# One mixer kernel on Trainium2: the convolution's first value and gate weights in turns, in four banks

## The chip, the cores and the metric

The kernel runs on one core of a Trainium2 chip. The metric is the device time of an execution in microseconds (us). The kernel before was run three times: median 685.47 us (684.65 to 685.96). A core has five engines that work side by side and wait for one another by semaphores: TensorE (PE in the profile; its weight loads are PEld), VectorE (DVE), ScalarE (ACT), GpSimd (POOL) and SyncE (SP), which issues the transfers here. Matmuls write into PSUM, a memory of eight banks; everything else lives in SBUF.

## The reference

One decoder block in float32 over 256 tokens of width 1024:

```python
h = rmsnorm(x, norm_mix_g)
x = x + parallel_mixer(h, ...)          # attention heads | Conformer convolution, one w_in, one w_out
h = rmsnorm(x, norm_mem_g)
x = x + memory_cross_attention(h, rmsnorm(mem, mem_norm_g), w_mq, w_mkv, w_mo)
h = rmsnorm(x, norm_ffn_g)
x = x + hierarchical_moe(h, ...)        # top-1 group, top-2 of its 8 experts; 32 experts in all
return rmsnorm(x, final_g)

def conformer_conv(u, b_glu, w_dw, b_dw, ln_g, ln_b):   # u = h @ w_in[:, OFF_C:], width 2 x 512
    a, gate = jnp.split(u + b_glu, 2, axis=-1)
    z = a * jax.nn.sigmoid(gate)
    z = depthwise_causal_conv(z, w_dw, width=31) + b_dw
    return jax.nn.silu(layernorm(z, ln_g, ln_b))
```

The convolution's inputs are two products of h, the value `a` and the gate, each 512 columns of `w_in`. The change is about the first half of these columns, chunk 0, at the very start of the kernel.

## The kernel before, in words

**Tiling.** The 256 tokens are two row blocks of 128. x is normalised block by block (`normed`): square sums on ScalarE (first half of the columns) and VectorE (second half), the reciprocal root, then the scaling, again half on ScalarE and half on VectorE, into `xn`. TensorE transposes `xn` into the tile `ht`, two rows j of the contraction at a time, and `put_split` takes it out of PSUM as two float32r parts: a high part (ScalarE) and a low part, the remainder (VectorE). The contraction of 1024 has eight such rows j. Every matrix product of the mixer is done in three matmuls (`mm3`, lines 414 to 417): high x high, high x low, low x high. Weights are split in the same way by `split`, two rows j a piece: the high part `WH` is a cast on ScalarE (line 409), the low part `WL` a subtraction (line 411), every third on VectorE, the others on POOL. Pieces have five buffers.

**Convolution.** `conv_chunk(c)` multiplies 256 value columns (tiles `pa`, two blocks b) and then 256 gate columns (`pg`) of one chunk, 48 matmuls each. Then ScalarE's sigmoid of the gate (line 534) and VectorE's product with the value (line 535) write `z`. The depthwise convolution runs on VectorE as 31 tap operations for each of four channel blocks, 124 in all (`conv_taps`, lines 507 to 516); the program hands them out between the other work by `some_taps`. After the last one `ysum` adds up the channel blocks; `ln_mean` (line 706) lets TensorE multiply it by ones for the LayerNorm's mean `mu`, and VectorE subtracts it (line 707). The LayerNorm's result enters the output projection (`xo`).

**What comes after.** The products for v (tile `pv`; VectorE takes eight columns of it into `fS`, line 554), q and k, attention, the keys of the memory (`pmk`), its values (`pmv`), the output projection, cross-attention, and the 32 experts in eight groups.

**Weights.** SyncE transfers them in tiles of 1 MB into a ring of buffers in a fixed order (`Ring`); a transfer is issued once its buffer has been freed by the work that read it. In the last two thirds of the run these are the experts' weights, about 192 MB.

**What sets the order.** The program is recorded and a scheduler sets each engine's order from priorities; `tc.high_priority(80)` around the splits lets them go ahead of work recorded up to 80 instructions earlier. Inside `tc.manual_schedule(engines=...)` the named engines keep the order in which the program is written. Each engine then works strictly in its order. `keep_warm` issues matmuls without a use (fillers), 16 of them at the start. PSUM's banks are shared out by tags: `mm` has three banks, `tr` (transposes) and `sc` two each, `acc` one.

Of the kernel before, what the change touches and what calls it, by code (L numbers as in the profile page):

```python
# [11 lines left out]
F32 = mybir.dt.float32  # L12
# [41 lines left out]
NSLOT3 = 2  # L54
NWARM = 13
NWARM2 = 5
NWARM0 = 16


class Ring:  # L60
# [3 lines left out]
    def __init__(self, tc):  # L64
        self.tc = tc
        self.nc = tc.nc
        self.size = {}
        self.first = 0
        self.held = 0
        self.begun = False  # L70
        self.todo = deque()
        self.free = deque()
        self.kept = deque()
        self.live = []
# [28 lines left out]
    def pump(self, limit=1000):  # L103
        while self.todo and limit:
            key, shape, src, within = self.todo[0]
            if within is None:
                pool = next((p for p in self.free if self.size[p] >= math.prod(shape)), None)
                if pool is None:
                    return
                self.free.remove(pool)  # L110
                v = self.view(pool, shape, F32)
                self.live.append((key, v, pool))
                v = v[:, :, :src.shape[2]]
            else:
                v = next(e[1] for e in self.live if e[0] == within[0])[:, :, within[1]]
            limit -= 1
            self.todo.popleft()

            n = 1 if self.begun else 2
            self.begun = True  # L120
            for k in range(0, shape[0], shape[0] // n):
                self.nc.sync.dma_start(v[:, k:k + shape[0] // n], src[:, k:k + shape[0] // n])

    def take(self, key):
        for e in self.live:
# [37 lines left out]
def body(tc, a, out):  # L163
# [31 lines left out]
    def tr_ps(name, shape=(P, 512)):  # L195
        return ps.tile(list(shape), F32, tag="tr", name=name, bufs=2)
# [78 lines left out]
    def qcols(key, view, c0, n):  # L275
        ring.queue(key, (NJ, n), view[:, :, c0:c0 + n])

    for c in range(2):
        qcols(("ca", c), winv, OFF_C + 256 * c, 256)
        qcols(("cg", c), winv, OFF_C + DC + 256 * c, 256)  # L280
    ring.queue(("mem", 0), (NT, D), mem.rearrange("(i p) d -> p i d", p=P))
    for c in range(2):
        qcols(("v", c), winv, OFF_V + VF * c, VF)
# [42 lines left out]
            c0, w = SLICES[2]  # L326
            ring.queue(None, (4, w), wv[:, 3, :, c0:c0 + w], (("ed3", 1), slice(256, 512)))

    ring.pump(2)
    prow = prec.tile([P, P], F32, name="prow")  # L330
    qrow = prec.tile([20, P], F32, name="qrow")
    nc.sync.dma_start(prow[0:124, :], a["w_dw"][0].rearrange("t (c p) -> (t c) p", p=P))
    nc.sync.dma_start(prow[124:128, :], a["b_dw"][0].rearrange("(c p) -> c p", p=P))
    nc.sync.dma_start(qrow[0:8, :], a["b_glu"][0].rearrange("(c p) -> c p", p=P))
    nc.sync.dma_start(qrow[8:12, :], a["conv_ln_g"][0].rearrange("(c p) -> c p", p=P))
    nc.sync.dma_start(qrow[12:16, :], a["conv_ln_b"][0].rearrange("(c p) -> c p", p=P))
    nc.sync.dma_start(qrow[16:20, :], a["attn_out_g"][0].rearrange("(c p) -> c p", p=P))
# [2 lines left out]
    ln_g = qTm[:, 8:12]  # L340
    ln_b = qTm[:, 12:16]
    ao_g = qTm[:, 16:20]
    gain("mem_norm_g", "(p k) -> p k", "mem_norm_g")
    ring.pump(4)
    nc.sync.dma_start(bfor, a["b_forget"][0].partition_broadcast(P))
    ring.first = 1000
    ring.pump()
# [49 lines left out]
    wsp = [None]  # L397
    nsplit = [0]

    def split(v):  # L400

        m = v.shape[2]
        n = 2 * VF // m
        for k in range(0, v.shape[1], n):
            src = v[:, k:k + n]
            with tc.high_priority(AHEAD):
                hi = wsp[0].tile([P, 2 * VF], F32R, tag="WH", name="WH")[:, :n * m].rearrange("p (a b) -> p a b", a=n)
                lo = wsp[0].tile([P, 2 * VF], F32R, tag="WL", name="WL")[:, :n * m].rearrange("p (a b) -> p a b", a=n)
                A.copy(hi, src)  # L409
                nsplit[0] += 1  # L410
                (V if nsplit[0] % 3 == 0 else G).tensor_tensor(lo, src, hi.bitcast(F32), op=OP.subtract)  # L411
            yield [(k + i, hi[:, i], lo[:, i]) for i in range(n)]

    def mm3(o, L, R, first, last):
# [22 lines left out]
    def blocked(k):  # L437
        return slice(k * P, (k + 1) * P)

    def normed(src, dst):  # L440

        for i in range(NT):
            ss = small.tile([P, 2], F32, tag="nrmss", name="nrmss")
            ssq(ss[:, 0:1], src[:, i, :D // 2], A)
            ssq(ss[:, 1:2], src[:, i, D // 2:], V)
            r = small.tile([P, 1], F32, tag="nrmr1", name="nrmr1")
            V.tensor_add(r, ss[:, 0:1], ss[:, 1:2])
            A.activation(r, r, AF.Sqrt, scale=1.0 / D, bias=eps_t)
            V.reciprocal(r, r)
            A.activation(dst[:, i, :D // 2], src[:, i, :D // 2], AF.Copy, scale=r)  # L450
            V.tensor_scalar(dst[:, i, D // 2:], src[:, i, D // 2:], r, None, op0=OP.mult)

    def wstat(key, pair, name, between={}, bank=mm_ps):

# [34 lines left out]
    wst = ExitStack()  # L489
    wsp[0] = wst.enter_context(tc.tile_pool(name="wsp", bufs=NPIECE, side="right", reuse_waits="tile"))  # L490

    normed(X, xn)
    transposed(hT, xn, gvec["norm_mix_g"], 0, NJ, strided, "h")
    ring.done(xn_pool)
    t = tr_ps("prm_t")
    T.transpose(t[:, 0:P], prow, ident)
    T.transpose(t[:, P:P + 20], qrow, ident[0:20, 0:20])
    V.tensor_copy(pT, t[:, 0:P])
    V.tensor_copy(qTm, t[:, P:P + 20])


    z = cvp.tile([P, 4, S + CW - 1], F32, name="z")
    V.memset(z[:, :, 0:CW - 1], 0.0)
# [21 lines left out]
        for _ in range(n):  # L525
            next(taps, None)

    def conv_chunk(c):
        pa = wstat(("ca", c), hT, "pa")
        pg = wstat(("cg", c), hT, "pg")  # L530
        for b in range(2):
            cb = 2 * c + b
            sg = cvp.tile([P, S], F32, tag="sg", name="sg", bufs=2)
            A.activation(sg, pg[b], AF.Sigmoid, bias=b_glu[:, 4 + cb:5 + cb])
            V.scalar_tensor_tensor(z[:, cb, CW - 1:], pa[b], b_glu[:, cb:cb + 1], sg, op0=OP.add, op1=OP.mult)

    conv_chunk(0)
    conv_chunk(1)
    exp_ln = A.preload_act_table_set("natural_log_exp_and_others")
    tc.keep_in_program_order(exp_ln)  # L540

# [835 lines left out]
```

## Time and profile before

| | |
|---|---|
| median of 3 runs | 685.47 us |
| the profiled execution | 686.98 us, its span 685.3 us |
| TensorE busy | 595.5 us, 87% of the span |
| VectorE busy | 224.2 us, 33%, nearly all of it in the first 260 us |
| ScalarE, POOL busy | 173.0 and 119.1 us |
| transfers | 237.35 MB, mean 346 GB/s |

The span is cut into 40 equal slices of 17.1 us in the page. Shares over the whole span say little here, since the mixer and cross-attention fill the first third and the experts the rest; the rows below are therefore taken from single stretches. In the timeline a row has the start, the busy time of the merged instructions, engine, line, operation, the tiles (out<-in), the shape and the count; in brackets stands how long the engine was idle before and what ended that. Matmul durations overlap, so the distance of their starts is what counts.

### The profile page before, as it was taken

The numbers are of one execution on the slowest core, as the hardware profiler recorded it, in microseconds if no ns is written. First come the engines' busy times: TensorE is split into PE (matmuls) and PEld (weight loads), VectorE is DVE, ScalarE is ACT, GpSimd is POOL, SyncE is SP. The second block draws the span as 40 slices with busy tenths as digits, with TensorE's granted clock in tenths as the row PEclk, the third lists the DMA queues.
The fourth block names the chain that finished last, engine by engine and source line by source line (L and its number), as shares of the span: only waits on it lengthen the run. The fifth ranks groups of instructions, "written<-read, shape, count | busy, mean of one in ns | idle before, by whom it ended". The sixth has DMA issues, their size and how long they took to land. (4 is left out here: it accounts for less than half of the span.)

```text
span 685.3 us, 8873 instructions
## 1 busy us (share of the span) xinstructions
PE 595.5 (87%) x3497; PEld 353.1 (52%) x3497; DVE 224.2 (33%) x489; ACT 173.0 (25%) x375; POOL 119.1 (17%) x106
## 2 busy tenths in 40 slices
PE   7999999998999999999768968976895788789775
PEld 5999889876998852625312612521261243125122
DVE  5699879887775630400000100000010000001013
ACT  6576675574654510000000000000000000000004
POOL 4546425674333200000000000000000000000000
PEclk9999999999999999999989989998999899899898
DMA  7979550555966999999999999999999999999993
GB/s 247 358 184 364 209 193 2 184 185 191 361 232 221 395 360 421 420 418 419 420 420 418 421 419 420 419 421 419 421 418 421 419 420 419 421 419 418 421 398 116
DMA packets 65163, 237.35 MB, mean 346 GB/s; under 512 B 11852, under 2 KB 31456, under 8 KB 42080
## 3 DMA queue, kind: packets, MB, share of 16 engines
q1 hardware_dynamic: 64832, 235.72, 87.6%
q10 hardware_dynamic: 288, 1.05, 0.4%
q8 instruction: 28, 0.46, 0.3%
q14 instruction: 15, 0.12, 0.0%
HBM read 235.70 MB, written 1.05 MB: 345 GB/s over the span
## 5 line engine op out<-in xcount | busy, mean ns | idle before, releaser
L1311 PE MATMUL eu<-w,tg 128*32 128x512 f32 x512 | 105.3, 715 | 43.9 <-DMA w<-in_w_up 43.9
L411 POOL TENSOR_TENSOR WL<-w,WH 128x512 fp32r<-128x512 f32 (+1 forms) x80 | 109.2, 1375 | 110.7 <-ACT WH L409 94.9
L1339 PE MATMUL ed<-w,hT 128*32 128x512 f32 x448 | 86.5, 597 | 15.4 <-DMA w<-in_w_down 10.6
L1311 PEld LDWEIGHTS eu<-w,tg 128*32 128x32 f32 x512 | 22.3, 126 | 123.0 <-DMA w<-in_w_up 78.8
L409 ACT CAST WH<-w 128x512 fp32r<-128x512 f32 (+1 forms) x120 | 72.9, 619 | 46.6 <-PE pmk L416 7.3
L998 POOL TENSOR_SCALAR SR<-S,r 128x128 f32<-128x128 f32 x7 | 4.2, 605 | 388.2 <-PE Y L1050 337.3
L1034 DVE TENSOR_TENSOR sgm<-sgm,eu 128x512 f32<-128x512 f32 x8 | 5.5, 688 | 192.7 <-PE eu L1311 164.6
L1016 PEld LDWEIGHTS tgp<-SR,X 128*128 128x128 f32 x256 | 62.0, 335 | 12.0 <-ACT SR L997 9.5
L1016 PE MATMUL tgp<-SR,X 128*128 128x128 f32 x256 | 63.8, 405 | 3.6 <-ACT SR L997 3.6
L1339 PEld LDWEIGHTS ed<-w,hT 128*32 128x32 f32 x448 | 22.2, 109 | 74.6 <-issue 37.4
L512 DVE SCALAR_TENSOR_TENSOR cacc<-z,pT,cacc 128x256 f32<-128x256 f32 x116 | 56.4, 486 | 2.6
L1311 PE MATMUL eg<-w,tg 128*32 128x512 f32 x448 | 53.8, 594 | 0.8 <-DMA w<-in_w_gate 0.8
L1004 DVE TENSOR_TENSOR S<-S,GT 128x256 f32<-128x256 f32 x8 | 3.4, 425 | 126.4 <-POOL SR L998 126.3
L1040 ACT COPY hT<-hTp 128x512 f32<-128x512 f32 x8 | 4.7, 586 | 152.2 <-PE hTp L1037 152.2
L411 DVE TENSOR_TENSOR WL<-w,WH 128x512 fp32r<-128x512 f32 (+1 forms) x40 | 36.4, 911 | 11.0 <-ACT WH L409 10.7
L1033 ACT ACTIVATE sgm<-eg 128x512 f32<-128x512 f32 x8 | 4.8, 597 | 128.3 <-PE eg L1311 112.2
L1311 PEld LDWEIGHTS eg<-w,tg 128*32 128x32 f32 x448 | 16.9, 109 | 30.6 <-issue 22.4
L1048 ACT COPY yd<-ed 128x512 f32<-128x512 f32 x14 | 8.2, 586 | 93.8 <-PE ed L1339 93.8
L1017 DVE TENSOR_TENSOR tg<-tgp,g_norm_ffn_g 128x512 f32<-128x512 f32 (+2 forms) x19 | 11.5, 607 | 53.0 <-PE tgp L1016 53.0
L1050 PE MATMUL Y<-yd,GST 128*128 128x512 f32 x56 | 25.9, 605 | 0.0
L415 PE MATMUL pmk<-w,WH 128*128 128x256 f32 x64 | 18.8, 294 | 0.0
L416 PE MATMUL pmk<-w,WH 128*128 128x256 f32 x64 | 18.5, 290 | 0.0
(353 smaller groups left out, 976.4 us busy)
## 6 DMA issues: line engine op xcount, KB each, us to landing
w<-in_w_gate SPq DMA_DIRECT2D x64, 1024.0 KB, 19.9
w<-in_w_up SPq DMA_DIRECT2D x64, 1024.0 KB, 19.9
w<-in_w_down SPq DMA_DIRECT2D x63, 1024.0 KB, 19.9
w<-in_w_mkv SPq DMA_DIRECT2D x8, 1024.0 KB, 12.8
w<-in_w_in SPq DMA_DIRECT2D x7, 1024.0 KB, 10.5
w<-in_w_out SPq DMA_DIRECT2D x4, 1024.0 KB, 9.4
w<-in_w_mq SPq DMA_DIRECT2D x4, 1024.0 KB, 13.2
w<-in_w_mo SPq DMA_DIRECT2D x4, 1024.0 KB, 5.5
```

The costliest lines, as they stand in the source:

```text
L409: A.copy(hi, src)
L411: (V if nsplit[0] % 3 == 0 else G).tensor_tensor(lo, src, hi.bitcast(F32), op=OP.subtract)
L415: T.matmul(o, L[0], R[0], start=first, stop=False)
L416: T.matmul(o, L[0], R[1], start=False, stop=False)
L512: V.scalar_tensor_tensor(dst, z[:, cb, t:t + S], pT[:, 4 * t + cb:4 * t + cb + 1], acc, op0=OP.mult, op1=OP.add)
L1016: T.matmul(t[:, j], X[:, i, ja + j::NJ], SR[:, i], start=i == 0, stop=i == NT - 1)
L1017: V.tensor_tensor(tg[:, ja:ja + step], t, gff[:, ja:ja + step].unsqueeze(2).to_broadcast([P, step, n]), op=OP.mult)
L1034: V.tensor_mul(sg, sg, pu[0:n])
L1048: ins = A.copy(yd[:, :w], pd[0:n, :w])
L1050: T.matmul(outs[i], GST[:, i], yd[:, :w], start=first, stop=last)
L1311: T.matmul(o[32 * q:32 * q + 32], tg[:, j, 32 * q:32 * q + 32], ws[q][0][:, jj], start=j == 0, stop=j == NJ - 1, tile_position=(0, 32 * q))
L1339: T.matmul(os_[n][32 * q:32 * q + 32], hh[:, j, 32 * q:32 * q + 32], ws[q][0][:, jj, 512 * n:512 * n + 512], start=j == 0, stop=j == 3, ti ...
```

## The change

It does the following.

- The first value and gate weights (`w0`, two ring buffers) are transferred ahead of the rest, each in three pieces of two, two and four rows j, in turns.
- `normed` works on one row block at a time. For block 0 the scaling of the first half of the columns goes from ScalarE to POOL. The sums of block 1 stand behind block 0's on ScalarE.
- On TensorE, VectorE and ScalarE the front is written out by hand: transposes of the first four rows j of block 0, three fillers (of 16; 13 stay at the start), the same of block 1, then pair by pair 12 matmuls of the value and 12 of the gate, each pair's transposes two pairs ahead. Both high parts of a pair precede both low parts (`h_split`). POOL isn't among the engines whose order is written out.
- Value and gate of chunk 0 have four banks (two `mm`, two `sc`). Their low parts go to POOL (value) and to VectorE (gate). Chunk 1's value takes one bank of `mm` and one of `tr`.
- The sigmoids and `z` of chunk 0 come after all 96 matmuls of the chunk.

```diff
-NWARM0 = 16
+NWARM0 = 13
...
-
-            n = 1 if self.begun else 2
-            self.begun = True
-            for k in range(0, shape[0], shape[0] // n):
-                self.nc.sync.dma_start(v[:, k:k + shape[0] // n], src[:, k:k + shape[0] // n])
+            self.nc.sync.dma_start(v, src)
     def take(self, key):
         for e in self.live:
...
     def qcols(key, view, c0, n):
         ring.queue(key, (NJ, n), view[:, :, c0:c0 + n])
-    for c in range(2):
-        qcols(("ca", c), winv, OFF_C + 256 * c, 256)
-        qcols(("cg", c), winv, OFF_C + DC + 256 * c, 256)
+
+    w0 = [ring.spare((NJ, 256)) for _ in range(2)]
+    for j0, j1 in ((0, 2), (2, 4), (4, 8)):
+        for (v, _), c0 in zip(w0, (OFF_C, OFF_C + DC)):
+            nc.sync.dma_start(v[:, j0:j1], winv[:, j0:j1, c0:c0 + 256])
+    for key, c0 in (("ca", OFF_C), ("cg", OFF_C + DC)):
+        qcols((key, 1), winv, c0 + 256, 256)
...
-    ring.pump(2)
+    ring.pump(1)
...
+    ring.pump(2)
-    ring.pump(4)
+    ring.pump(2)
...
-    def split(v):
+    def split(v, eng=None):
...
-                (V if nsplit[0] % 3 == 0 else G).tensor_tensor(lo, src, hi.bitcast(F32), op=OP.subtract)
+                (eng or (V if nsplit[0] % 3 == 0 else G)).tensor_tensor(lo, src, hi.bitcast(F32), op=OP.subtract)
...
-    def normed(src, dst):
-
-        for i in range(NT):
-            ss = small.tile([P, 2], F32, tag="nrmss", name="nrmss")
-            ssq(ss[:, 0:1], src[:, i, :D // 2], A)
-            ssq(ss[:, 1:2], src[:, i, D // 2:], V)
-            r = small.tile([P, 1], F32, tag="nrmr1", name="nrmr1")
-            V.tensor_add(r, ss[:, 0:1], ss[:, 1:2])
-            A.activation(r, r, AF.Sqrt, scale=1.0 / D, bias=eps_t)
-            V.reciprocal(r, r)
-            A.activation(dst[:, i, :D // 2], src[:, i, :D // 2], AF.Copy, scale=r)
-            V.tensor_scalar(dst[:, i, D // 2:], src[:, i, D // 2:], r, None, op0=OP.mult)
+    def normed(i):
+
+        ss = small.tile([P, 2], F32, tag="nrmss", name="nrmss")
+        ssq(ss[:, 0:1], X[:, i, :D // 2], A)
+        ssq(ss[:, 1:2], X[:, i, D // 2:], V)
+        r = small.tile([P, 1], F32, tag="nrmr1", name="nrmr1")
+        V.tensor_add(r, ss[:, 0:1], ss[:, 1:2])
+        A.activation(r, r, AF.Sqrt, scale=1.0 / D, bias=eps_t)
+        V.reciprocal(r, r)
+        if i == 0:
+            G.tensor_scalar(xn[:, i, :D // 2], X[:, i, :D // 2], r, None, op0=OP.mult)
+        else:
+            A.activation(xn[:, i, :D // 2], X[:, i, :D // 2], AF.Copy, scale=r)
...
-    normed(X, xn)
-    transposed(hT, xn, gvec["norm_mix_g"], 0, NJ, strided, "h")
-    ring.done(xn_pool)
-    t = tr_ps("prm_t")
-    T.transpose(t[:, 0:P], prow, ident)
-    T.transpose(t[:, P:P + 20], qrow, ident[0:20, 0:20])
-    V.tensor_copy(pT, t[:, 0:P])
-    V.tensor_copy(qTm, t[:, P:P + 20])
-
     z = cvp.tile([P, 4, S + CW - 1], F32, name="z")
     V.memset(z[:, :, 0:CW - 1], 0.0)
...
-    def conv_chunk(c):
-        pa = wstat(("ca", c), hT, "pa")
-        pg = wstat(("cg", c), hT, "pg")
+    def conv_glu(c, pa, pg):
         for b in range(2):
             cb = 2 * c + b
             sg = cvp.tile([P, S], F32, tag="sg", name="sg", bufs=2)
             A.activation(sg, pg[b], AF.Sigmoid, bias=b_glu[:, 4 + cb:5 + cb])
             V.scalar_tensor_tensor(z[:, cb, CW - 1:], pa[b], b_glu[:, cb:cb + 1], sg, op0=OP.add, op1=OP.mult)
-    conv_chunk(0)
-    conv_chunk(1)
+
+    ht = [None] * (NJ // 2)
+
+    def h_transposes(i, m):
+        if i == 0:
+            ht[m] = tr_ps("ht", (P, 2, S))
+        for kk in range(2):
+            T.transpose(ht[m][:, kk, i * P:(i + 1) * P], xn[:, i, strided(2 * m + kk)], ident)
+
+    def h_split(m):
+        g = gvec["norm_mix_g"]
+        ks = [(kk, 2 * m + kk) for kk in range(2)]
+        for kk, k in ks:
+            A.activation(hT.hi(k), ht[m][:, kk], AF.Copy, scale=g[:, k:k + 1])
+        for kk, k in ks:
+            V.scalar_tensor_tensor(hT.lo(k), ht[m][:, kk], g[:, k:k + 1], hT.hi(k).bitcast(F32),
+                                   op0=OP.mult, op1=OP.subtract)
+
+    def products(o, piece):
+        for b in range(2):
+            bs = slice(b * P, (b + 1) * P)
+            for j, hi, lo in piece:
+                mm3(o[b], (hi[:, bs], lo[:, bs]), hT.both(j), j == 0, j == NJ - 1)
+
+    ET = mybir.EngineType
+    with tc.manual_schedule(engines={ET.PE, ET.Activation, ET.DVE}):
+        normed(0)
+        for m in range(2):
+            h_transposes(0, m)
+        keep_warm(onesb, 3)
+        normed(1)
+        sa, sb = split(w0[0][0], G), split(w0[1][0], V)
+        ap = next(sa)
+        for m in range(2):
+            h_transposes(1, m)
+        pa = [mm_ps("pa", (P, S)) for _ in range(2)]
+        pg = [sc_ps("pg", (P, S)) for _ in range(2)]
+        h_split(0)
+        for m in range(NJ // 2):
+            bp = next(sb)
+            products(pa, ap)
+            if m < NJ // 2 - 1:
+                h_split(m + 1)
+                ap = next(sa)
+            products(pg, bp)
+            if m + 2 < NJ // 2:
+                for i in range(NT):
+                    h_transposes(i, m + 2)
+        t = tr_ps("prm_t")
+        T.transpose(t[:, 0:P], prow, ident)
+        T.transpose(t[:, P:P + 20], qrow, ident[0:20, 0:20])
+        V.tensor_copy(qTm, t[:, P:P + 20])
+        V.tensor_copy(pT, t[:, 0:P])
+        conv_glu(0, pa, pg)
+        ring.done(xn_pool, w0[0][1], w0[1][1])
+
+    banks = cycle((mm_ps, tr_ps))
+    pa = wstat(("ca", 1), hT, "pa", bank=lambda name, shape: next(banks)(name, shape))
```

Where the scheduler and the new code move instructions is seen from the engines' orders. POOL at the start; `WL` is a low part of weights, `w<-X,nrmr` the scaled half of x, `BR` and `iotag` small tables. Before:

```order
L225 CAST Ub<-U 128x128
L249 MEMSET BR 128x40
L252 IOTA iotag 128x32
L411 TENSOR_TENSOR WL<-w,WH 128x512 x11
L411 TENSOR_TENSOR WL<-w,WH 128x520 x5
```

After the change, the same place on POOL:

```order
L220 CAST Ub<-U 128x128
L411 TENSOR_TENSOR WL<-w,WH 128x512
L244 MEMSET BR 128x40
L247 IOTA iotag 128x32
L450 TENSOR_SCALAR w<-X,nrmr_238 128x512
L411 TENSOR_TENSOR WL<-w,WH 128x512 x8
```

One low part of the weights moved ahead of the two tables and stands ahead of the new scaling of block 0. TensorE's first transposes wait for that scaling.

VectorE at the end of the taps, from the last three low parts to the subtraction of the mean; `cacc` and `y<-z,pT,cacc` are taps, `pmv` the memory's values. Before:

```order
L512 SCALAR_TENSOR_TENSOR cacc<-z,pT,cacc 128x256 x7
L411 TENSOR_TENSOR WL<-w,WH 128x512
L512 SCALAR_TENSOR_TENSOR cacc<-z,pT,cacc 128x256 x6
L411 TENSOR_TENSOR WL<-w,WH 128x512
L512 SCALAR_TENSOR_TENSOR y<-z,pT,cacc 128x256
L515 TENSOR_TENSOR ysum<-ysum,y 128x256
L730 COPY w<-pmv 128x512
L411 TENSOR_TENSOR WL<-w,WH 128x512
L707 SCALAR_TENSOR_TENSOR y<-mu,y 128x1024
```

After:

```order
L505 SCALAR_TENSOR_TENSOR cacc<-z,pT,cacc 128x256 x7
L411 TENSOR_TENSOR WL<-w,WH 128x512
L505 SCALAR_TENSOR_TENSOR cacc<-z,pT,cacc 128x256 x5
L778 COPY w<-pmv 128x512
L505 SCALAR_TENSOR_TENSOR cacc<-z,pT,cacc 128x256
L411 TENSOR_TENSOR WL<-w,WH 128x512
L505 SCALAR_TENSOR_TENSOR cacc<-z,pT,cacc 128x256 x2
L505 SCALAR_TENSOR_TENSOR y<-z,pT,cacc 128x256
L508 TENSOR_TENSOR ysum<-ysum,y 128x256
L755 SCALAR_TENSOR_TENSOR y<-mu,y 128x1024
```

The second low part of the upper piece is the first of the lower one. Up to it the order has 123 taps before and 115 after; behind it stand nine taps instead of one, and the copy of `pmv` and a low part moved ahead of `ysum`. Between the first `z` and the first `fS` the count of taps is 39 before and 31 after, and there is one low part less. On TensorE the order from the first product of chunk 1 on is the same in both kernels, but for one matmul.

## Rows read from the trace of the kernel before

**Rows 1.** The page's 40 slices: GB/s of all transfers.

```profile
GB/s 247 358 184 364 209 193 2 184 185 191 361 232 221 395 360 421 420 418 419 420 420 418 421 419 420 419 421 419 421 418 421 419 420 419 421 419 418 421 398 116
```

**Rows 2.** Windows: stretch, length, each engine's busy us (count), PEclk, DMA share, GB/s.

```profile
210.00:215.00 5.00, 5.00 (x29) 4.28 (x28) 2.90 (x6) 3.29 (x8) 2.59 (x2) 1.00 0.33 128
```

**Rows 3.** Waits of SyncE's queue: for whom, us in total, times, longest.

```profile
SPq L122 <- PE eg L1290: 16.8, 4, 8.3
```

**Rows 4.** Waits of TensorE, 26 to 260 us: us in total, times, longest.

```profile
PE xo L417 <- DVE w L720: 1.5, 1, 1.5
PE pq L415 <- DVE fS L554: 0.7, 1, 0.7
```

**Rows 5.** Timeline of the front, four engines: start us, busy us, engine, instruction.

```profile
7.08 0.16 DVE L447 TENSOR_TENSOR nrmr<-nrmss 128x1 f32<-128x1 f32 x1 [0.27 <-ACT junkA L382]
...
8.42 1.12 ACT L409 CAST WH<-w 128x512 fp32r<-128x512 f32 x2
...
9.11 4.21 POOL L411 TENSOR_TENSOR WL<-w,WH 128x512 fp32r<-128x512 f32 x3 [6.33 <-ACT WH L409]
...
9.97 0.50 PE L415 MATMUL pa<-w,WH 128*128 128x256 f32 x2 [0.34 <-ACT w L421]
```

**Rows 6.** Groups by form on POOL: count, busy us, mean ns, idle before.

```profile
L998 POOL TENSOR_SCALAR SR<-S,r 128x128 f32<-128x128 f32 x7 | 4.2, 605 | 388.2 <-PE Y L1050 337.3 <-PE pn L1070 50.9
```

**Rows 7.** Timeline of TensorE: fillers, and transposes at the lower clock.

```profile
1.18 5.92 PE L232 MATMUL warm<-onesb 128*128 128x512 bf16 x16 [1.18 <-POOL onesb L227]
...
12.72 1.09 PE L430 MATMUL ht<-ident,w 128*128 128x128 f32 x4 [0.85 <-DVE w L422]
```

**Rows 8.** Windows: the stretch of the lower clock (PEclk is third from the end).

```profile
12.50:16.50 4.00, 3.78 (x20) 3.81 (x21) 2.55 (x5) 2.40 (x6) 2.09 (x2) 0.57 0.65 192
```

**Rows 9.** Timeline of ScalarE: table load and sigmoid.

```profile
21.15 1.28 ACT L534 ACT_TABLE_LOAD   x1
23.41 0.47 ACT L534 ACTIVATE sg<-pg,qTm 128x256 f32<-128x256 f32 x1 [0.97 <-PE pg L417]
```

**Rows 10.** Timeline: the first z, the gate's second block, the first product of v.

```profile
23.92 0.48 DVE L535 SCALAR_TENSOR_TENSOR z<-pa,qTm,sg 128x256 f32<-128x256 f32 x1 [2.06 <-ACT sg L534]
...
23.93 0.38 PE L415 MATMUL pg<-w,WH 128*128 128x256 f32 x1 [0.56 <-ACT sg L534]
...
39.22 0.28 PE L415 MATMUL pv<-WH,w 128*128 128x260 f32 x1
```

**Rows 11.** Windows: 30 products at the full clock.

```profile
29.21:32.74 3.53, 3.53 (x32) 3.53 (x31) 3.39 (x8) 1.59 (x3) 2.44 (x3) 1.00 1.09 349
```

**Rows 12.** Timeline of VectorE: fS, two waits, the end of the taps.

```profile
52.24 0.17 DVE L554 TENSOR_TENSOR fS<-pv,bfor 128x8 f32<-128x8 f32 x1
...
76.72 0.48 DVE L422 SCALAR_TENSOR_TENSOR w<-mt,g_mem_norm_g,w 128x256 fp32r<-128x256 f32 x1 [2.28 <-ACT w L421]
...
110.60 0.69 DVE L411 TENSOR_TENSOR WL<-w,WH 128x512 fp32r<-128x512 f32 x1 [0.31 <-ACT WH L409]
...
122.31 3.63 DVE L512 SCALAR_TENSOR_TENSOR cacc<-z,pT,cacc 128x256 f32<-128x256 f32 x7
...
129.60 1.25 DVE L411 TENSOR_TENSOR WL<-w,WH 128x512 fp32r<-128x512 f32 x1
...
131.28 1.01 DVE L515 TENSOR_TENSOR ysum<-ysum,y 128x256 f32<-128x256 f32 x1
...
132.82 0.68 DVE L411 TENSOR_TENSOR WL<-w,WH 128x512 fp32r<-128x512 f32 x1
```

**Rows 13.** Groups by form on VectorE, 24 to 53 us: low parts.

```profile
L411 DVE TENSOR_TENSOR WL<-w,WH 128x512 fp32r<-128x512 f32 x3 | 3.1, 1028 | 0.4 <-ACT WH L409 0.4
```

**Rows 14.** Timeline of TensorE: the mean.

```profile
133.62 0.59 PE L706 MATMUL mu<-ysum,ones 128*128 128x256 f32 x2
```

**Rows 15.** Windows: the lower and the full clock behind the LayerNorm.

```profile
161.00:162.00 1.00, 1.00 (x4) 0.71 (x3) 1.00 (x3) 0.52 (x1) 0.41 (x1) 0.50 0.95 315
164.00:165.00 1.00, 1.00 (x6) 0.81 (x5) 0.67 (x1) 0.27 (x1) 0.00 (x0) 1.00 1.05 410
```

More of the change, by code (lines that the diff above doesn't have):

```diff
@@ L69, in __init__ @@
         self.held = 0
-        self.begun = False
         self.todo = deque()
@@ L438, in blocked @@
         return slice(k * P, (k + 1) * P)
-    def normed(src, dst):
-        for i in range(NT):
-            ss = small.tile([P, 2], F32, tag="nrmss", name="nrmss")
-            ssq(ss[:, 0:1], src[:, i, :D // 2], A)
-            ssq(ss[:, 1:2], src[:, i, D // 2:], V)
-            r = small.tile([P, 1], F32, tag="nrmr1", name="nrmr1")
-            V.tensor_add(r, ss[:, 0:1], ss[:, 1:2])
-            A.activation(r, r, AF.Sqrt, scale=1.0 / D, bias=eps_t)
-            V.reciprocal(r, r)
-            A.activation(dst[:, i, :D // 2], src[:, i, :D // 2], AF.Copy, scale=r)
-            V.tensor_scalar(dst[:, i, D // 2:], src[:, i, D // 2:], r, None, op0=OP.mult)
+    def normed(i):
[10 more added lines that the diff above has]
+            A.activation(xn[:, i, :D // 2], X[:, i, :D // 2], AF.Copy, scale=r)
+        V.tensor_scalar(xn[:, i, D // 2:], X[:, i, D // 2:], r, None, op0=OP.mult)
     def wstat(key, pair, name, between={}, bank=mm_ps):
@@ L535, in conv_chunk @@
             V.scalar_tensor_tensor(z[:, cb, CW - 1:], pa[b], b_glu[:, cb:cb + 1], sg, op0=OP.add, op1=OP.mult)
-    conv_chunk(0)
-    conv_chunk(1)
+    ht = [None] * (NJ // 2)
[50 more added lines that the diff above has]
+    pa = wstat(("ca", 1), hT, "pa", bank=lambda name, shape: next(banks)(name, shape))
+    conv_glu(1, pa, wstat(("cg", 1), hT, "pg"))
     exp_ln = A.preload_act_table_set("natural_log_exp_and_others")
```

## The prediction

> **What bounds the kernel now.** I read the page's slices first. From about 255 us to the end the transfers run at their ceiling, about 420 GB/s [rows 1]: there the expert weights decide, and nothing in this change touches them. Before that they are not at the ceiling: between 210 and 215 us they are busy a third of the time [rows 2], because the next weights wait for a buffer that TensorE has yet to free (16.8 us in four waits for its first expert matmuls alone [rows 3]). So a delay of TensorE ahead of 210 us moves every later transfer by as much and arrives at the end in full, and so does a gain. The question is when TensorE gets through the mixer. The next view is what TensorE waits for between 26 and 260 us: very little, and the largest waits are for VectorE [rows 4]. VectorE is the second bound of the mixer: it carries 124 tap operations of the depthwise convolution between its other work, and the LayerNorm behind them ends in the 1.5 us wait.
>
> **The front, up to the first product.** Before, the first product starts at 9.97 us [rows 5]. In the change ScalarE skips one half of the normalisation of row block 0, so its square sum of block 1 starts earlier. VectorE waited 0.27 us for that sum at 7.08 [rows 5], and that is about all that can come earlier: 0.25 us. The first cast (8.42) comes at 8.17, and the low part on POOL (9.11) at 8.86. On POOL this low part now stands ahead of the half that was moved there from ScalarE. So the moved multiplication cannot begin before 8.86 + 1.4 (4.21 us for three [rows 5]) = 10.3, and all transposes of block 0 wait for it. No row has a 128x512 multiplication by a scalar on POOL. Low bound 0.6 us, the one of 128x128 [rows 6]; high bound four times that, 2.4. I take 1.4, the low part of the same size. So block 0 is ready at 11.7 (10.9 to 12.7). The Trainium skill, GPSIMD Engine Reference, 4.1 Engine selection, says that a one-input operation runs there roughly at line rate and a two-input one about half as fast; an estimate from that and the low part's row is 0.7 us, and the sum would be 0.7 us smaller. No row here shows it.
>
> Then TensorE does four transposes, three fillers, four transposes. The fillers are 13 + 3 now. The first 13 end at 1.2 + 13 x 0.37 = 6.0 [rows 7], so TensorE idles 5.7 us. Before, shorter gaps were enough to bring the granted clock to its lower level (1.2 GHz) for most of the 4 us behind 12.5 [rows 8]; I count the restart at that level. Four transposes 1.1 [rows 7], three fillers 1.1, two transposes 0.55, ScalarE's high part 0.5 (the sigmoid's row, of the same shape [rows 9]) and 0.1 of hand-over: 3.3 us, so the first product starts at 15.0, 5.0 us later than before.
>
> **The convolution's first chunk.** Before, from the first product to the first of v it takes 39.22 - 9.97 = 29.25 us [rows 5, 10], though 192 products need only 192 x 0.118 = 22.7 (30 of them in 3.53 us at full clock [rows 11]). The rest are the other transposes, waits for high and low parts, the lower clock, and once in each chunk the wait for a sigmoid that holds the gate's bank (0.56 us shown [rows 10], with the restart about 0.8). The change takes these away: in four banks value and gate alternate by pairs of rows, each pair's high and low part is made during the other's products, and chunk 1 has banks of its own. After: 96 products 11.3, eight transposes 1.1 (half the time of rows 7's each, at full clock), 0.4 for the low part that the first pair waits for (VectorE now makes it second), 0.4 for the rest of the lower clock (0 to 1.2). Chunk 0 ends at 28.2, and v begins 0.3 + 11.3 us later at 39.8, against 39.22. TensorE itself loses only 0.6 us: the stalls removed pay for most of the late start.
>
> **What is late next: VectorE.** Before, the gate b=0 was finished ahead of b=1, so the first z came at 23.92 [rows 10], in the middle of chunk 0. Now both gates end together at 28.2, and behind them come a cast 0.6 [rows 5], a table load 1.3 and a sigmoid 0.5 [rows 9]: z at 30.6, 6.7 us later, and the taps start with it. The order answers by putting taps later. Up to the first fS it has 31 of them where there were 39, and one low part less. A tap takes 3.63/7 = 0.52 us [rows 12], a low part 1.0 [rows 13]. So fS comes 6.7 - 4.1 - 1.0 = 1.6 us later than 52.24 [rows 12]. TensorE waits there already (0.7 us [rows 4]), because fS frees the bank of its next matmul, so this replaces the 0.6: +1.6 at 52 us.
>
> From there VectorE is tied to TensorE and ScalarE again: it waits 2.28 us at 76.7 and 0.31 at 110.6 [rows 12], and since TensorE is 1.6 us late too, those waits remain. The eight taps stay behind. At the low part of 129.60 [rows 12] the order has 115 taps done instead of 123. Behind it stood one tap, the sum ysum, a copy of pmv and a low part; now stand eight more taps, and copy and low part are ahead of the sum. So ysum ends 8 x 0.52 + 1.2 (copy and low part, which ended at 133.5) = 5.3 us later than its 132.29 [rows 12], relative to TensorE. TensorE multiplies it into the mean at 133.62 [rows 14], at a fixed place in its order, with 1.3 us to spare before: it will stand still 4.0 us. Nothing gives that back: the chain from the mean to the LayerNorm's end runs through VectorE and ends in the 1.5 us wait [rows 4], which moves with it.
>
> A stop of 4 us should also lower the clock. Behind the waits for the LayerNorm the granted clock was at the lower level in 161 to 162, four matmuls per us instead of six [rows 15]. At that ratio a low stretch of 3 to 4 us costs 1.0 to 1.3, at half rate 1.7; some of it hides in the later wait for the LayerNorm, so I take 1.0 (0 to 1.7).
>
> **Sum.** Front and fS +1.6, the mean +4.0, the clock +1.0: +6.6 us. The profiled execution took 686.98 us (span 685.3); with it 693.6. It lies 1.5 above the median of 685.47, and the difference carries over: 692.1. The moved DMAs (six pieces instead of three issues ahead of the small tables) cost nothing: the first piece is cast at 8.17 behind ScalarE's own work, the rest is needed after 15; if one came late, the first pair would wait by that much.
>
> **Rivals.**
> VectorE catches up (the other side): it makes up the eight taps in the waits that it still has (2.28 and 0.31 us shown [rows 12], more between), so fS and ysum come in time. Decided by whether ysum ends within 1.3 us of its place; then only TensorE's own 0.6 is left, 686.1, no change. For it: the waits are there. Against: the order is fixed, and a wait ahead of a listed instruction can't be filled by a later tap. 0.11.
>
> The low part doesn't hold POOL's half up, and the front works: first product some 3.5 us earlier, at 11.5. Then z comes at 27.1 and fS 1.9 us earlier than before; but the mean still waits 4.0, since that lag is set by the order and not by the start: 685.5 - 1.9 + 4.0 = 687.6, with the clock 688.6. For it: POOL was idle until 9.11 [rows 5]. Against: POOL's order shows the low part first. 0.12.
>
> The clock stays low longer: 3.5 us more of chunk 0 at half rate add 1.7, and the stop at the mean costs the full 1.7, so 0.7 more: 694.5. For it: the gap of 5.7 us is longer than any that the front had. Against: by the mean of 0.57 over 12.5 to 16.5 [rows 8] the clock was nearly back at the end of that stretch. The Trainium skill, TensorE: Matmul & The Clock Gate, Why this matters for your kernels, warns of idle gaps between bursts of matmuls; on that the trace agrees [rows 8, 15], and this rival is its rule taken at its worst. 0.12.
>
> The forecast: 692.1, own range 690 to 693.5. 0.62. The remaining 0.03 is a gain that I don't see.
>
> **Range and chances.** The forecast's terms with their bounds (block 0 0.8 earlier to 1.0 later, each clock term from 0, the mean 3.5 to 4.7) and most of the second and third rivals give 687.5 to 694.5; the first rival lies outside. About 0.2% (1.4 us) is what a measurement of this kernel can tell from no change. Slower by more than that: 0.62 + 0.12 + 0.12, less a hundredth, 0.85; within it: most of the first rival, 0.10; faster: 0.05.
>
> **What would show it.** In the profile of the changed kernel: POOL's multiplication by nrmr at about 10.3, behind a low part; the first product near 15; no sigmoid wait at the gates; the first z near 30.6; a longer wait for fS near 54; and above all the mean's matmul waiting about 4 us for ysum near 135, with VectorE doing taps right up to it. I am wrong if that wait is under 1 us, or if the transposes of block 0 start by 7 us.

## The result, and the profile after

The changed kernel took 694.55 us (median of 4 runs, 693.64 to 696.43) against 685.72 us for the kernel before on the same chip: ratio 1.0133, 95% interval 1.0106 to 1.0159. It is slower, as forecast, and by more: 692.1 us was predicted, with 694.5 as the upper end. A second session (e1 below) gave 693.15 us and 1.0107 (1.0079 to 1.0136). The executions of one kernel differ by 4 to 6 us, so the two sessions don't contradict each other; the median of all 13 executions of the changed kernel is 694.0. Within a session the changed kernel lies 7.5 to 8.8 us above the kernel before.

The profiled execution took 693.64 us, its span 691.9. In the order of the prediction's steps: the front on POOL and then on TensorE (start us, busy us, engine, instruction, idle time before it and what ended it), which answer [rows 5].

```profile
8.91 1.26 POOL L411 TENSOR_TENSOR WL<-w,WH 128x512 fp32r<-128x512 f32 x1 [6.31 <-ACT WH L409]
10.11 0.13 POOL L244 MEMSET BR<- 128x40 f32 x1
10.19 0.17 POOL L247 IOTA iotag<- 128x32 f32 x1
10.35 1.57 POOL L450 TENSOR_SCALAR w<-X,nrmr 128x512 f32<-128x512 f32 x1
```

```profile
11.97 1.12 PE L535 MATMUL ht<-ident,w 128*128 128x128 f32 x4 [5.55 <-POOL w L450]
12.88 1.48 PE L227 MATMUL warm<-onesb 128*128 128x512 bf16 x3
14.16 1.06 PE L535 MATMUL ht<-ident,w 128*128 128x128 f32 x4
15.36 0.58 PE L415 MATMUL pa<-w,WH 128*128 128x256 f32 x1
```

The low part stands ahead of the scaling on POOL, and all of TensorE's front waits for that scaling. Next, the first z (23.92 before [rows 10]) and fS on VectorE (52.24 before [rows 12]), and the wait for fS on TensorE (0.7 us before [rows 4]).

```profile
31.06 0.48 DVE L526 SCALAR_TENSOR_TENSOR z<-pa,qTm,sg 128x256 f32<-128x256 f32 x1 [1.04 <-ACT sg L525]
```

```profile
54.39 0.17 DVE L602 TENSOR_TENSOR fS<-pv,bfor 128x8 f32<-128x8 f32 x1
```

```profile
54.61 0.39 PE L415 MATMUL pq<-w,WH 128*128 128x256 f32 x1 [1.66 <-DVE fS L602]
```

The end of the taps on VectorE, and the mean on TensorE, which answer [rows 12, 14].

```profile
139.05 0.74 DVE L411 TENSOR_TENSOR WL<-w,WH 128x512 fp32r<-128x512 f32 x1
139.71 1.00 DVE L505 SCALAR_TENSOR_TENSOR cacc<-z,pT,cacc 128x256 f32<-128x256 f32 x2
140.75 0.48 DVE L505 SCALAR_TENSOR_TENSOR y<-z,pT,cacc 128x256 f32<-128x256 f32 x1
141.26 0.42 DVE L508 TENSOR_TENSOR ysum<-ysum,y 128x256 f32<-128x256 f32 x1
```

```profile
136.85 0.40 PE L417 MATMUL pmv<-WH,w 128*128 128x512 f32 x1
141.74 0.70 PE L754 MATMUL mu<-ysum,ones 128*128 128x256 f32 x2 [4.50 <-DVE ysum L508]
```

VectorE works right up to ysum, and TensorE stands still for it: 133.62 before, 141.74 now. Last, windows of TensorE (stretch, length, busy us and count, then PEclk, DMA share, GB/s), which answer [rows 8, 15].

```profile
12.00:16.00 4.00, 3.80 (x12) 0.50 1.10 327
78.00:82.00 4.00, 4.00 (x25) 0.64 0.00 0
142.00:146.00 4.00, 4.00 (x12) 0.57 0.00 0
166.00:170.00 4.00, 2.52 (x11) 1.00 0.26 54
170.00:174.00 4.00, 3.72 (x19) 1.00 0.98 374
```

The lower level (1.2 GHz) stands behind the first wait (12 to 16) and behind the mean's (142 to 146), where a wait stands ahead. It also stands near 78, where TensorE had not waited since 54.6; no step of the prediction had that. At 166 to 174, around the LayerNorm's wait (1.48 us, over at 167.90), the clock is full; in the kernel before that wait ended at 159.09 and a low stretch stood behind it.

The milestones of the traces, each the start of that product in us, with the time of the same execution (pa: the first value product; cps: the first small product behind those for q; pk: the last of those for k; mu: the mean; pp: L1011, see below):

| trace | first pa | first cps | last pk | mu | pp | time |
|---|---|---|---|---|---|---|
| before | 9.97 | 57.52 | 82.32 | 133.62 | 241.32 | 686.98 |
| changed | 15.36 | 59.54 | 85.76 | 141.74 | 249.05 | 693.64 |
| e1 (changed) | 15.23 | 59.42 | 85.66 | 141.65 | 248.91 | 693.29 |
| e14 (changed) | 15.44 | 61.36 | 86.16 | 142.11 | 249.80 | 695.67 |
| e15 (changed) | 15.42 | 61.22 | 86.02 | 141.98 | 249.55 | 694.01 |
| e16 (changed) | 15.40 | 59.60 | 85.79 | 141.76 | 248.94 | 693.05 |
| e2 | 10.16 | 54.35 | 82.07 | 138.04 | 245.29 | 690.50 |
| e3 | 15.22 | 61.49 | 88.47 | 142.92 | 250.04 | 695.29 |
| e4 | 11.64 | 55.83 | 84.34 | 138.77 | 246.59 | 690.62 |
| e5 | 15.37 | 61.77 | 88.00 | 139.55 | 246.11 | 689.98 |
| e6 | 10.03 | 56.65 | 81.45 | 136.08 | 243.86 | 689.12 |
| e7 | 15.27 | 59.56 | 84.28 | 136.90 | 244.40 | 690.36 |
| e8 | 10.28 | 54.39 | 79.17 | 130.97 | 238.58 | 684.09 |
| e9 | 9.51 | 53.71 | 79.93 | 135.89 | 243.12 | 687.90 |
| e10 | 15.44 | 59.64 | 84.44 | 140.39 | 248.11 | 695.96 |
| e11 | 9.96 | 56.38 | 82.60 | 134.15 | 241.20 | 687.29 |
| e12 | 10.31 | 54.54 | 80.85 | 132.64 | 240.25 | 685.26 |
| e13 | 9.62 | 53.70 | 79.92 | 131.76 | 239.23 | 683.42 |

pp is one of the last products ahead of the expert stage. Up to it the changed kernel loses 7.6 to 8.5 us in its five traces, against the one trace of the kernel before; the medians differ by about 8.

### The profile page after: what moved, and what is told of

Same layout as the page of the kernel before. It is cut to its first block, busy times and chain, and to the rows that moved or that the text cites. A ratio compares the mean times of both kernels' runs of the same rounds, so it can differ in the third digit from the quotient of the medians.

```text
span 691.9 us, 8882 instructions
## 1 busy us (share of the span) xinstructions
PE 596.2 (86%) x3497; PEld 353.6 (51%) x3497; DVE 225.8 (33%) x491; ACT 171.9 (25%) x374; POOL 117.2 (17%) x105
## 5 line engine op out<-in xcount | busy, mean ns | idle before, releaser
L1359 PE MATMUL eu<-w,tg 128*32 128x512 f32 x512 | 102.5, 701 | 42.1 <-DMA w<-in_w_up 42.1
L411 POOL TENSOR_TENSOR WL<-w,WH 128x512 fp32r<-128x512 f32 (+1 forms) x78 | 105.7, 1364 | 120.9 <-ACT WH L409 114.1
L1387 PE MATMUL ed<-w,hT 128*32 128x512 f32 x448 | 89.6, 597 | 16.0 <-DMA w<-in_w_down 11.3
L411 DVE TENSOR_TENSOR WL<-w,WH 128x512 fp32r<-128x512 f32 (+1 forms) x42 | 39.0, 934 | 8.2 <-ACT WH L409 7.7
L1359 PEld LDWEIGHTS eg<-w,tg 128*32 128x32 f32 x448 | 17.0, 109 | 30.6 <-issue 22.3
```

The source lines that it names most:

```text
L411: (eng or (V if nsplit[0] % 3 == 0 else G)).tensor_tensor(lo, src, hi.bitcast(F32), op=OP.subtract)
L1359: T.matmul(o[32 * q:32 * q + 32], tg[:, j, 32 * q:32 * q + 32], ws[q][0][:, jj], start=j == 0, stop=j == NJ - 1, tile_position=(0, 32 * q))
L1387: T.matmul(os_[n][32 * q:32 * q + 32], hh[:, j, 32 * q:32 * q + 32], ws[q][0][:, jj, 512 * n:512 * n + 512], start=j == 0, stop=j == 3, ti ...
```

## The experiments

Times are medians, ratios those to the kernel before in the same session. Where kernels of different sessions are compared, the ratios are the safer measure.

**e1, the changed kernel again.**

> The changed kernel once more, unchanged. My theory (late front, fS 2 us later, mu stall 4.5 us, and stretches at the lower clock that come and go): 694.6 us, within 693.6 to 696.5, ratio 1.0125 to 1.0140; the milestones of the profile repeat (first product 15.4, first z 31.1, mu wait 4.5), while the low-clock stretches of the mixer (77.6 to 80.8, 142 to 146) may stand elsewhere, and the time of a run falls with its mean granted clock by about 1 us for each 0.01. Rival (the 77 us stretch belongs to the change): it stands at the same place again.

693.15 us, 1.0107 (1.0079 to 1.0136), a little below my range. The low clock at 77 came again at the same place, as the rival says; e14 and e15 below lack it, and e11, with the old front, has it, so it comes without the change too, and not always with it.

**e2, only POOL's order at the front.**

```
-    with tc.manual_schedule(engines={ET.PE, ET.Activation, ET.DVE}):
+    with tc.manual_schedule(engines={ET.PE, ET.Activation, ET.DVE, ET.Pool}):
```

> Only GpSimd's order at the front is changed: the scaling of block 0 (L450) stands ahead of the first low part. Theory (what the front lost is the scaling behind the low part): L450 starts at 5.7 instead of 10.35, the first product near 10.7 instead of 15.4, first z near 26.4 instead of 31.1, chunk-1 pa near 24.3; this passes to fS and on, the order of the taps on VectorE is the same, so the mu wait stays 4 to 4.5 us: 694.6 - 4.4 = 690.2 us (689 to 691.5). Rival A (the front is the whole loss): 686 us or less, mu wait under 1 us. Rival B (the four banks with the late sigmoids are the loss, the scaling only fills idle time): under 1 us gained, 693.6 us or more.

689.77 us, 1.0050 (1.0029 to 1.0070): 3.4 faster than e1, and the trace's pp 3.6 earlier. The scaling now comes first:

```profile
5.59 2.37 POOL L450 TENSOR_SCALAR w<-X,nrmr 128x512 f32<-128x512 f32 x1 [2.81 <-DVE nrmr L448]
8.96 1.27 POOL L411 TENSOR_TENSOR WL<-w,WH 128x512 fp32r<-128x512 f32 x1 [1.00 <-ACT WH L409]
```

First product 10.16, first cps 5.1 us earlier than in e1, and yet the mean waits the same (waits of TensorE: us in total, times, longest):

```profile
PE mu L754 <- DVE ysum L508: 4.5, 1, 4.5
```

So the mean's wait does not come from the late z as such. It comes from VectorE's order, which has 25 taps behind the scalings of att (L751) in both kernels, 17 before the change.

**e9, the scaling back on ScalarE.**

```
-        if i == 0:
-            G.tensor_scalar(xn[:, i, :D // 2], X[:, i, :D // 2], r, None, op0=OP.mult)
-        else:
+        if True:
             A.activation(xn[:, i, :D // 2], X[:, i, :D // 2], AF.Copy, scale=r)
```

> The changed kernel with one part undone: block 0's scaling is on ScalarE again, all else (two turns, four banks, order of the loads) as changed. Theory (what the front lost is the scaling in GpSimd's order, not the turns): block 0's transposes start near 6.5 us, the first product near 10.5 instead of 15.4; as e2, 690 us (688.5 to 691.5), the mu wait stays 4.5. Rival (the turns and banks are the loss): 693 us or more.

687.43 us, 1.0016 (1.0003 to 1.0029), below my range. The scaling is over at 6.3 on ScalarE, and block 0's transposes start at 6.68:

```profile
5.60 0.72 ACT L450 ACTIVATE w<-X,nrmr 128x512 f32<-128x512 f32 x1 [0.23 <-DVE nrmr L448]
6.68 0.60 PE L533 MATMUL ht<-ident,w 128*128 128x128 f32 x4
9.51 0.39 PE L415 MATMUL pa<-w,WH 128*128 128x256 f32 x1 [0.34 <-ACT w L539]
```

This one part is worth 6.6 us of the 8 (694.0 less 687.43; by the ratios 6.2 to 8.0). Its order alone is worth 3.4 (e2). Against e2 it gains 0.64 at the first cps; the rest between their traces lies around 70 to 77, where e2's low clock cost 2.9 us and e9's 1.4 (from cps to the last pk, 27.72 and 26.22 against 24.80 before). The mean still waits 4.5. That the loss is nearly gone all the same has its reason ahead of it: e9's first cps stands at 53.71, where e6, the old front at full clock, has 56.65. So in these traces the new front is quicker once its scaling is cured, and the mean's wait takes that back.

**e5, eight taps less; e6, eight more in the kernel before.** In e5 block 3 has 23 taps instead of 31, in e6 it has 39.

```
-        for t in range(1, CW):
+        for t in range(9 if cb == 3 else 1, CW):      # e5, in the changed kernel
+        for t in range(-7 if cb == 3 else 1, CW):     # e6, in the kernel before
+            t = max(t, 1)
```

> The changed kernel with 8 of the 31 taps of the convolution's last block left out (16 taps instead of 24 to 25 behind the scalings of att on VectorE), nothing else. Theory (the mu stall is 8 taps of late VectorE work and sits on the chain to the end): mu wait 4.5 -> 0.3 us, the low clock behind it goes; 693.9 (median of the changed kernel's ten runs) - 4.3 = 689.6 us (688.5 to 691). Rival (the stall only shifts idle time from a later wait, the chain is bound elsewhere): 693 us or more.

> The kernel before with 8 taps more in the convolution's last block (tap 1 is taken 8 times more; 25 taps instead of 17 behind the scalings of att), the front untouched. Theory: this alone makes the mu wait about 4 us and costs 685.6 + 4.1 = 689.7 us (688.5 to 691), half of what the change costs. Rival (the old order has slack there, or the loss belongs to the new front): under 687 us.

e5: 689.89 us, 1.0060 (1.0038 to 1.0081), 4.1 under the changed kernel's 694.0 (by the ratios 3.2 to 5.0). The mean follows the products without a wait:

```profile
139.32 0.40 PE L417 MATMUL pmv<-WH,w 128*128 128x512 f32 x1
139.55 0.59 PE L754 MATMUL mu<-ysum,ones 128*128 128x256 f32 x2
```

e6: 689.40 us, 1.0057 (1.0035 to 1.0080), 3.3 above the kernel before in its session:

```profile
136.08 0.48 PE L707 MATMUL mu<-ysum,ones 128*128 128x256 f32 x1 [3.18 <-DVE ysum L516]
```

Eight taps behind that point cost 3.3 us in the old front and about 4.1 in the new. Both rivals fall.

**e3, 15 taps a stage, and e4, with e2's edit.**

```
-NTAP = 12
+NTAP = 15
```

> Only the number of taps queued per stage is changed, 12 to 15; VectorE then has 17 taps behind the scalings of att (as before the change) instead of 25, and the front stays. Theory (ysum is late by 8 taps of 0.52 us, and the stall then costs clock): the mu wait falls from 4.5 to about 0.3 us, first product stays at 15.4, fS at 54.4: 694.6 - 4.2 and up to 1 more of clock = 690 us (689 to 691.5). Rival (VectorE's order is not what binds, ysum waits for the front itself): mu wait stays above 3 us, 693.5 us or more. Rival (the clock is the loss): 692 to 694 with the wait gone but the low clock elsewhere.

> Both edits, GpSimd's order at the front and 15 taps a stage. Theory: the two gains add, 694.6 - 4.4 - 4.6 = 685.6 us (684 to 687.5), first product near 10.7, mu wait under 1 us. Rival (they are one loss, each alone gives it all back): 690. Rival (the four banks cost something by themselves): 688 or more.

Both missed: e3 696.23 us, 1.0150 (1.0123 to 1.0176), e4 689.45 us, 1.0053 (1.0034 to 1.0071).

```profile
PE mu L754 <- DVE ysum L508: 2.3, 1, 2.3
```

In e3 the mean's wait halved (e4's is the same 2.3), but the last pk came at 88.47 and mu at 142.92, later than in any trace of the changed kernel. By VectorE's order 40 taps instead of 33 now stand between the first attention scores and the scalings of att, so part of the delay has moved ahead of the mean. The other traces price it. e14 has e3's low clock to 20 but none at 78: from the first cps to the last pk e3 takes 2.2 us more (26.98 against 24.80), of which the stretch at 78 is 1.4, and from there to mu 1.5 less. e4 against e2 shows the same 0.8 more and 1.5 less. So 15 taps a stage bring the mean only 0.7 us earlier. That e3's median lies 3.1 above e1's is not explained by this: up to pp its trace is 1.1 later than e1's. e4 came out at the numbers of its two rivals (690; 688 or more), but both fall with e8 and e13 below, which keep the four banks and are faster: 15 taps a stage had cured little of the mean's delay.

**e7, fillers in the wait for fS, and e10, more fillers at the start.**

```
+    keep_warm(onesb, 8)        # e7: ahead of the first q product
-NWARM0 = 13
+NWARM0 = 28                    # e10
```

> The changed kernel with 8 filler products of 512 columns on TensorE ahead of the first q product, where it waits 1.7 us for fS; by the order VectorE then has 21 taps, not 25, behind the scalings of att, so the mu wait falls too, to 2.4 us. Theory A (the idle time near 54 us brings the low clock at 77 us): that stretch goes, from the first cps to the last pk 24.4 us as before the change instead of 25.9; 693.9 - 1.4 - 2.1 = 690.4 us (689 to 691.5). Theory B (the low clock at 77 comes from the small sp and ncp products ahead of it): the stretch stays, 691.8 us.

> The changed kernel with 28 filler products at the start instead of 13, so that TensorE is busy in the 5.6 us in which it waits for the scaling. Theory (the low clock behind that wait costs 1 us in the quick and 3 in the slow executions): granted clock 1.00 from 12 to 20 us, first product near 14.2 instead of 15.4, 693.9 - 1.5 = 692.4 us (691 to 693.2), and less spread. Rival (the clock at the front costs nothing in the end, since fS binds behind it): 693.5 us or more. If the fillers last past 12 us they cost what they last longer.

e7: 692.04 us, 1.0088 (1.0058 to 1.0118). The low clock at 77 was gone in its trace, as theory A says, and the mean's wait was 1.1; the median lies above A's range, near B's price. But e10 (693.28 us, 1.0100, 1.0070 to 1.0130) takes theory A's evidence away: it waited 1.6 us for fS and has no low clock at 77 either (windows of TensorE in e10):

```profile
74.00:78.00 4.00, 4.00 (x29) 1.00 0.06 21
78.00:82.00 4.00, 4.00 (x36) 1.00 0.00 0
```

e10 misses its own aim: its fillers ended at 9.2, TensorE still waited 2.8 us for the scaling, the clock fell at 12, and the first product came at 15.44.

**e8, the low parts behind the front on POOL; e11, the same in the kernel before; e12, with fillers; e13, with the scaling on ScalarE.**

```
-                (eng or (V if nsplit[0] % 3 == 0 else G)).tensor_tensor(lo, ...)
+                (eng or (V if nsplit[0] % 100 == 0 else G)).tensor_tensor(lo, ...)
```

With 100, one low part behind the front (near 185 us) stays on VectorE in e8 and e13. e8 has e2's edit too, e13 e9's, and e12 is e8 with `keep_warm(onesb, 6)` at the place of e7's.

> GpSimd's order at the front as in e2, and all low parts behind the front on GpSimd (before: each third on VectorE); 15 taps stand behind the scalings of att instead of 25. Theory: against e2 (689.8) the mu wait of 4.5 us goes: 685.3 us (683.5 to 686.5), which would be no slower than the kernel before. Rival (GpSimd becomes late: products of wo and mv wait for WL): 688 us or more, with waits for POOL's L411 on TensorE of some us.

> The kernel before with all low parts on GpSimd (in the first chunks too), the edit that e8 has beside GpSimd's order at the front. Theory (before has no mu wait to take away, so this edit is worth little there, and e8's gain comes from the new front): 685.2 us (684 to 686.5). Rival (the edit is the whole gain of e8): 683.5 to 684.3 us. Rival (GpSimd too slow for the first chunks, 1.40 us a low part): 687 us or more.

> e8 with 6 filler products ahead of the first q product, where TensorE waited 1.5 us for fS. Theory: they take up the wait and cost nothing, no low clock at 70 to 77 in any execution: 683.8 us (682.8 to 685), at least as quick as e8 (684.2). Rival (the fillers push the q products): 685 us or more.

> The changed kernel with block 0's scaling on ScalarE (as e9) and all low parts behind the front on GpSimd (as e8): both losses cured, the turns and the four banks kept. Theory: e9 (687.4) less the mu wait of 4.5, of which e8 got 5.6 against e2: 683.3 us (682 to 684.5), first product 9.5, no mu wait; 2.7 under e11 (686.0), the kernel before with the same low parts, which is then what turns and banks gain. Rival (turns and banks gain nothing): 685.5 us or more.

| kernel | us | ratio to before |
|---|---|---|
| e8 | 684.16 | 0.9976 (0.9956 to 0.9996) |
| e13 | 683.67 | 0.9978 (0.9957 to 1.0000) |
| e12 | 685.32 | 0.9984 (0.9968 to 1.0001) |
| e11 | 685.99 | 0.9991 (0.9977 to 1.0005) |

VectorE has 15 taps behind the scalings of att now in e8 and e13 (12 in e12), and ysum is ready 4 us ahead of the mean (e13, VectorE, then TensorE):

```profile
126.70 0.62 DVE L506 TENSOR_TENSOR ysum<-ysum,y 128x256 f32<-128x256 f32 x1
```

```profile
131.76 0.59 PE L752 MATMUL mu<-ysum,ones 128*128 128x256 f32 x2
```

So with the scaling and the mean's wait cured, turns and banks are no loss. e8 is the only one whose whole interval lies below 1, and only by 0.04%. Whether turns and banks gain anything over e11 stays open: in the traces e13's pp is 2.0 us earlier, but the intervals overlap. e12 missed its range by 0.3 us, and it ends theory A: its fillers run from 46.97 right up to the first q product and leave 0.2 us of the wait for fS, and a low clock at 72 to 76 is there, which e8's trace doesn't have (rows, then windows of TensorE):

```profile
46.97 1.47 PE L227 MATMUL warm<-onesb 128*128 128x512 bf16 x6
49.34 0.39 PE L415 MATMUL pq<-w,WH 128*128 128x256 f32 x1 [0.20 <-DVE fS L602]
```

```profile
46.00:50.00 4.00, 3.80 (x27) 1.00 1.08 360
70.00:74.00 4.00, 4.00 (x26) 0.80 1.04 386
74.00:78.00 4.00, 4.00 (x29) 0.78 0.59 219
```

**e14 to e16, the changed kernel three times more, one execution each.**

> The changed kernel again, one look. Theory (the slow executions lose it in the front): if the granted clock is back at 1.00 by 16 us, the first cps stands near 59.5 and the time is 692 to 694; if it stays low to 20, the first cps stands near 61.6 and the time is 695 to 697. Rival (the expert stage makes the spread): the time does not go with the first cps.

> As e14: time 692 to 694 with the first cps near 59.5, 695 to 697 with it near 61.6; or, by the rival, no such tie.

> As e14: time 692 to 694 with the first cps near 59.5, 695 to 697 with it near 61.6; or, by the rival, no such tie.

695.67, 694.01 and 693.05 us. Windows of TensorE in e14, then in e16:

```profile
16.00:20.00 4.00, 3.70 (x18) 0.50 1.07 386
78.00:82.00 4.00, 4.00 (x33) 1.00 0.00 0
```

```profile
16.00:20.00 4.00, 3.71 (x31) 1.00 1.06 384
78.00:82.00 4.00, 4.00 (x27) 0.70 0.00 0
```

The first cps stands at 61.4 and 61.2 where the low clock lasted to about 20, and at 59.4 to 59.6 in the other three; that part came as expected. But the time goes with it poorly (694.01 in e15, where 695 to 697 was expected), since the two with the longer stretch have no low clock at 77: at the mean all five stand within 0.5 us (141.65 to 142.11). From pp to the end the five take 444.1 to 445.9 us, while pp itself differs by 0.9. So in these five more of the spread arises in the expert stage than ahead of it: the rival holds.

## Why the prediction was wrong in size and right in cause

- **What bounds.** Right. A delay ahead of the experts reaches the end: in all 18 traces pp stands between 238.6 and 250.0 us, and from there to the end it takes 443.9 to 447.9 us whether pp is early or late. e5 and e6 show it for the mean's wait alone. In this pair of traces it was 7.7 us at pp and 6.7 at the end.
- **The front.** Right. Scaling at 10.35 (10.3 predicted), 1.57 us (1.4), transposes at 11.97 (11.7), first product 15.36 (15.0). The Trainium skill, GPSIMD Engine Reference, 4.1 Engine selection, has one-input operations there at about line rate; the trace disagrees, since the one-input scaling took 1.57 us and the two-input low part 1.26. The estimate of 0.7 us worked out from that rule falls.
- **Chunk 0 and v.** The sigmoid waits are gone, and v starts at 40.34 instead of 39.8: the late start cost TensorE 1.1 us, not 0.6.
- **fS.** z at 31.06 (30.6). From 52.24 [rows 12] to 54.39, so +2.15 where +1.6 was predicted; the first cps shows +2.0.
- **The mean.** The mechanism is right: late ysum, a fixed place in TensorE's order, 4.5 us of wait for 4.0. e5 and e6 price it at 4.1 and 3.3.
- **The clock.** +1.0 was about right in sum and wrong in place. From cps to the last pk the trace loses 1.4 us at 77 (26.22 against 24.80), where no step had it. Behind the mean the low stretch stands as predicted (142.31 to 145.72, products 0.43 us apart instead of 0.23), but at the LayerNorm's wait the kernel before had its own low stretch [rows 15], which the changed one lacks: from mu to pp 107.31 us after, 107.70 before.
- **The rivals.** VectorE did not catch up. The rival that the front works needed POOL's other order: e2 gave it that and took 689.8, where its price was 687.6 to 688.6; e9, with the scaling off POOL, took 687.4. The rival of the longer low clock occurred in e14 and e15 and cost its 1.7 us at the first cps (1.8 in e14); about 1.4 came back at 77.
- **The step that failed** is the last of the sum: "It lies 1.5 above the median of 685.47, and the difference carries over: 692.1." It did not carry over. The changed kernel's profiled execution, 693.64, lies 0.4 below the median of its 13 executions, not 1.5 above. Taking off the 1.5 comes to adding the terms, 6.6, to the median, and that is too little for two reasons that the runs show. First, the terms were mis-sized: up to pp this pair of traces differs by 7.7, of which the mean is 0.5 over its 4.0 and fS 0.5 over its 1.6. Second, they were counted from an execution with a low clock at 12.5 to 16.5 [rows 8], which the kernel before doesn't always have: e6, with the same front, had the full clock there (1.00 in 12 to 16) and its first cps 0.9 earlier. The changed kernel has a low clock in the front in all five traces. 7.7 and 0.9 are 8.6, and on 685.5 they give 694.1, where the median of its 13 executions stands (694.0). That the sum met the profiled execution (693.6 against 693.64) was luck: the 1.1 that it lacked at pp came back in the expert stage, which took 444.59 us there and 445.66 in the kernel before. Whether that stage was long by chance stays open: with the old front it took 445.26 (e6) and 446.09 (e11), in all 18 traces 443.9 to 447.9.

## What to carry to other kernels

An engine's order is a wait that no dependency shows: a scaling given to an idle GpSimd cost over 6 us, 3.4 of them because a low part stood ahead of it, and the cure is to look at the order of the engine that takes the work, not at how busy it is. A later stall can be set by the order alone: making the front 5 us earlier left the mean's wait at 4.5. And a difference between two profiled executions holds each one's own luck with the clock: before terms counted from one profile are added to a median, several profiles show which of its low stretches come every time.

## What the runs showed of the hardware

- The granted clock fell to its lower level during or right behind the 16 products of 8 rows (ncp, 74.29 to 77.0 in the changed kernel), with no wait of TensorE since 54.6. The stretch was there in 11 of 18 traces, between 70 and 83 us, and cost 1.4 or 2.9 us. It comes with waits for fS of 0.2 to 1.7 us and is missing with 0 to 1.65. The 16 products are in all 18 traces, so they alone don't bring it either. The changed kernel's five traces have it where the front's low clock ended by 16, and not where that lasted to 20; e3 and e5, with the same front, had both. Its cause stays open. The Trainium skill, TensorE: Matmul & The Clock Gate, Why this matters for your kernels, names idle gaps between bursts of matmuls; the stretches behind the front's wait and behind the mean agree with it, this one has no such gap.
- The same 128x512 scaling on GpSimd took 1.57 us with VectorE idle (10.35) and 2.37 us beside VectorE's work (5.59, in e2). The Trainium skill, GPSIMD Engine Reference, 1. Specifications, says that the two share their SBUF interfaces; the trace agrees, without showing that this is the reason.
